# One 128-row tile of a store sent as sixteen eight-partition stores, and the closing store cut in two

## The chip, the cores and the metric

The kernel runs on one core of a Trainium2 chip. The metric is the time of one execution on the device in microseconds (us), taken from executions that are not profiled. A separate, profiled execution gave the profile and its trace; times inside it are counted from the start of its span.

## The reference

For sixteen batches the output is a scaled product plus an addend, all in float32:

```python
batch, m, k, n = 16, 512, 1024, 768
x: (16, 512, 1024)   weight: (1024, 768)   scale: 0.1   add_value: (16, 512, 768)

def reference(x, weight, scale, add_value):
    return (scale * np.matmul(x, weight) + add_value).astype(np.float32)
```

Flattened, that is 8192 rows of x against one weight matrix. The kernel moves 33.6 MB of x, 25.2 MB of addend, 3.1 MB of weight and 25.2 MB of output.

## The kernel before

**Tiles.** The 8192 rows are 64 tiles of 128 rows. Row `g*2048 + p*16 + t` lies on partition `p` of tile `16*g + t`, so that n neighbouring tiles of one group of sixteen are, on each partition, one contiguous run in DRAM: 3072 B of output or addend for each tile, 4096 B of x. The function `rows(view, s, n)` gives that slice for tiles s to s+n-1.

**Buffers.** `xs` holds 16 tiles of x. `ao` holds 32 tiles in which the addend arrives and in which the output is formed in place; tile t lies in slot `(t + 8) % 32`, so that tiles 56 to 63 take the slots of tiles 24 to 31. `mm` is four PSUM tiles.

**Compute.** ScalarE and GpSimd (`mover`, line 147) cast x to bf16 in blocks, into two buffers `va` of four tiles each. VectorE (`turn`, line 162) transposes them into `xt`, two tiles at a time. TensorE (`product`, lines 195 and 197) multiplies each tile in eight steps of K. VectorE (`finish`, line 171) takes a pair of products from PSUM, scales them, adds the addend and writes the result to `ao`; it adds 2 to the semaphore `made`. VectorE works through groups of eight tiles, four pairs each; the last group is written out behind the loop.

**Transfers.** All DMAs are issued by SyncE's queue (SP), in the order that the list `STREAM` gives: `("x", s, n)` loads n tiles of x from tile s on, `"a"` the addend, `"w"` the weight, and `"o"` stores the output. Ahead of each transfer SP waits for what that transfer needs:

- an x load waits until ScalarE and GpSimd have moved the tiles whose slots it overwrites (`by_act`, `by_pool`);
- an addend load that begins a group of eight waits for the addend load before it (`a_sem`), and one that overwrites slots of the output waits until that store has landed (`o_sem`, line 115);
- a store waits for the store two ahead of it, and for `made` (lines 125 and 126).

The store of the last eight tiles stands outside the list, at line 237, behind the critical section that holds everything else:

```python
    s, n = LAST
    nc.sync.dma_start(rows(out_v, s, n), ao[:, slot(s):slot(s) + n, :])
```

The order of work around the change is therefore the order of `STREAM`, written out by hand: one queue, served in order by the core's 16 DMA engines.

Of the kernel before, what the change touches and what calls it, by code (L numbers as in the profile page):

```python
# [8 lines left out]
P = 128  # L9
# [18 lines left out]
]  # L28
FIRST, LAST = (0, 8), (56, 8)


@with_exitstack
def kernel(
# [17 lines left out]
    T = M // P  # L51
# [5 lines left out]
    out_v = out_f.rearrange("(g p t) n -> p g t n", p=P, t=R)  # L57
    w_v = weight.rearrange("(c p r) n -> p c (r n)", p=P, r=2)

    def rows(view, s, n):  # L60
        assert s // R == (s + n - 1) // R
        return view[:, s // R, s % R:s % R + n, :]
# [5 lines left out]
    ao = const.tile([P, A_SLOTS, N], fp32, name="ao")  # L68
# [6 lines left out]
    x_sem = [tc.alloc_semaphore(f"x{i}") for i in range(X_SLOTS // MOVE)]  # L75
    a_sem, a_late = (tc.alloc_semaphore(n) for n in ("a", "a_late"))
    o_sem = [tc.alloc_semaphore(f"o{i}") for i in range(2)]
    by_act, by_pool, pool_go, turned, casts, done, made = (
        tc.alloc_semaphore(name)
        for name in ("by_act", "by_pool", "pool_go", "turned", "casts", "done", "made"))  # L80
    TURNED = MOVE * VA_BUFS
    MADE = TURNED + 2 + MM_BUFS - 2

    def slot(t):
        return (t + G) % A_SLOTS

    def sync_engine(eng):
        loads, stores, known = [], [], {}

        def need(sem, value):  # L90
            if known.get(sem, 0) < value:
                eng.wait_ge(sem, value)
                known[sem] = value

        for op, s, n in STREAM:
            last = s + n - 1
            if op == "w":
                dst = ao[:, s:s + n, :].rearrange("p (c r) n -> p c (r n)", r=2)
                move, sem = eng.dma_start(dst, w_v[:, s // 2:(s + n) // 2, :]), w_sem[s // 4]
            elif op == "x":  # L100
                k = s % X_SLOTS
                if last >= X_SLOTS:
                    moved = 8 * (last + 1 - X_SLOTS) // MOVE
                    need(by_act, moved)
                    need(by_pool, moved)
                move = eng.dma_start(xs[:, k:k + n, :], rows(x_v, s, n))
                sem = x_sem[k // MOVE]
            elif op == "a":
                if loads and s % G == 0:
                    need(a_sem, 16 * len(loads))  # L110
                if slot(s) == 0:
                    need(casts, KJ)
                if s >= A_SLOTS:
                    i = next(j for j, (a, b) in enumerate(stores) if a <= s - A_SLOTS < a + b)
                    need(o_sem[i % 2], 16 * (i // 2 + 1))
                move = eng.dma_start(ao[:, slot(s):slot(s) + n, :], rows(add_v, s, n))
                if s % G:
                    sem = a_late
                else:
                    sem = a_sem  # L120
                    loads.append((s, n))
            else:
                i = len(stores)
                if i > 1:
                    need(o_sem[i % 2], 16 * (i // 2))
                need(made, MADE + last + 1)
                move = eng.dma_start(rows(out_v, s, n), ao[:, slot(s):slot(s) + n, :])
                sem = o_sem[i % 2]
                stores.append((s, n))
            move.then_inc(sem, 16)  # L130
            if op == "x" and n == 2 * MOVE:
                eng.sem_inc(x_sem[k // MOVE + 1], 16)
# [90 lines left out]
    s, n = FIRST  # L223
# [4 lines left out]
    with tc.tile_critical(no_gpsimd_drain=True):  # L228
        sync_engine(nc.sync)
        mover(nc.scalar, nc.scalar.copy, 0, by_act)  # L230
        nc.scalar.addr_align(HALF_BLOCK, offset=PAST)
        mover(nc.gpsimd, nc.gpsimd.tensor_copy, 1, by_pool, pool_go)
        nc.gpsimd.addr_align(HALF_BLOCK, offset=PAST)
        vector_engine(nc.vector)
        tensor_engine(nc.tensor)
    s, n = LAST
# [36 lines left out]
```

## Time and profile before

| What | Value |
|---|---|
| Time, median of 3 runs | 209.35 us (209.29 to 209.39) |
| Profiled execution, span from its first to its last instruction | 207.5 us |
| Median of the runs less that span | 1.85 us |
| Bytes moved by DMA | 87.06 MB, 420 GB/s over the span |
| TensorE matmul, busy | 168.4 us, 81% of the span |
| ScalarE, GpSimd, VectorE, busy | 134.7, 135.4, 97.8 us |
| Mean granted TensorE clock | 0.975 |

The profile gives no time of its own for the profiled execution other than its span. The 1.85 us between the span and the median lie around the span (start and end of an execution); the text takes them as fixed, so that an end that moves by d in the trace is taken to move the time by d.

How to read it: busy times are of the engine, without its waits. A matmul row's time is modelled, so a busy TensorE is not TensorE at its peak. The DMA share is the mean busy share of the 16 DMA engines; a row of a table by windows counts a DMA packet wholly in the window in which it starts, so that a share can exceed 1. "us to landing" counts from the issue of a DMA to its last completion.

### The profile page before, as it was taken

What the parts mean: (1) busy time and instruction counts of PE and PEld (TensorE: products, weight loads), DVE (VectorE), ACT (ScalarE), POOL (GpSimd) and SP (SyncE); (2) the same over time, 40 slices, a digit from 0 to 9 for tenths busy, and PEclk for the clock granted to TensorE, in tenths of its full rate; (3) what the DMA queues carried; (4) which work ended last, traced back from release to release, by engine and by line L of the source; (5) the groups of instructions that cost most, each with busy time, mean ns of one, the idle gap of its engine ahead of it and who ended that gap; (6) DMA issues with size and microseconds to landing.
All of it is one profiled execution on the core that took longest, in us unless ns stands there. A gap on an engine that the chain in (4) does not pass through costs nothing.

```text
span 207.5 us, 2310 instructions
## 1 busy us (share of the span) xinstructions
PE 168.4 (81%) x1024; PEld 50.3 (24%) x512; DVE 97.8 (47%) x66; ACT 134.7 (65%) x129; POOL 135.4 (65%) x132
## 2 busy tenths in 40 slices
PE   0000099999999999999999999999999999999400
PEld 0000023333332222222233333333333333333100
DVE  0005525537555555555555554755555555553300
ACT  2059970799999796969696079999970999300000
POOL 0049994799999996969696079999990899400000
PEclk9999999999999999999999999999999999999955
DMA  7999999999999999999999999999999999999993
GB/s 291 417 381 469 403 466 404 455 455 404 404 467 442 411 398 486 393 441 407 445 436 423 423 436 455 411 445 412 441 414 422 437 445 455 460 417 388 412 441 171
DMA packets 4147, 87.06 MB, mean 420 GB/s; under 512 B 432, under 2 KB 432, under 8 KB 944
## 3 DMA queue, kind: packets, MB, share of 16 engines
q1 hardware_dynamic: 4144, 87.03, 98.1%
q14 instruction: 3, 0.02, 0.0%
HBM read 61.87 MB, written 25.17 MB: 419 GB/s over the span
## 4 chain that ended last, share of the span: by engine, by line
PE 81%; DMA 6%; ACT 5%; DVE 1%; issue 1%; DVEq 0%; ACTq 0%
PE mm L197 81%; DMA xs<-in_x_dram 6%; ACT va L147 5%; DVE ao L171 1%; DVE xt L162 1%; ACTq L140 0%; DVEq L160 0%; DVEq L168 0%
## 5 line engine op out<-in xcount | busy, mean ns | idle before, releaser
L197 PE MATMUL mm<-w_bf,xt 128*128 128x512 bf16 (+1 forms) x1024 | 168.4, 328 | 26.0 <-DVE xt L162 26.0
L147 POOL CAST va<-xs 32x1024 bf16<-32x1024 f32 x128 | 135.2, 1056 | 43.1 <-DMA xs<-in_x_dram 24.7
L147 ACT CAST va<-xs 32x1024 bf16<-32x1024 f32 x128 | 133.4, 1042 | 42.1 <-DMA xs<-in_x_dram 25.8
L171 DVE SCALAR_TENSOR_TENSOR ao<-mm,ao 128x1536 f32 (+1 forms) x32 | 56.3, 1758 | 76.5 <-PE mm L197 76.5
L195 PEld LDWEIGHTS <-xt 128*128 128x128 bf16 x512 | 50.3, 98 | 143.6 <-issue 117.6
L162 DVE STREAM_TRANSPOSE xt<-va 128x1024 f32<-128x1024 f32 x32 | 39.4, 1234 | 3.8 <-ACT va L147 2.1
L155 DVE CAST w_bf<-ao 128x3072 bf16<-128x3072 f32 x2 | 4.5, 2240 | 18.1 <-DMA ao<-in_weight_dram 18.1
L136 ACT ACT_TABLE_LOAD x1 | 1.3, 1283 | 1.3 <-SPq L228 1.3
L254 POOL MEMSET const-float32-0.0<- 128x1 f32 x1 | 0.1, 98 | 0.2 <-issue 0.2
L254 POOL MEMSET const-bfloat16-1.0<- 128x1 bf16 x1 | 0.1, 100 | 0.0
L254 POOL MEMSET const-float32-1.0<- 128x1 f32 x1 | 0.1, 98 | 0.0
L254 POOL MEMSET const-uint8-127<- 128x1 uint8 x1 | 0.1, 97 | 0.0
## 6 DMA issues: line engine op xcount, KB each, us to landing
xs<-in_x_dram SPq DMA_DIRECT2D x7, 4096.0 KB, 20.9
ao<-in_add_value_dram SPq DMA_DIRECT2D x7, 3072.0 KB, 17.0
out_dram<-ao SPq DMA_DIRECT2D x6, 3072.0 KB, 27.0
out_dram<-ao SPq DMA_DIRECT2D x1, 6144.0 KB, 35.4
xs<-in_x_dram SPq DMA_DIRECT2D x2, 2048.0 KB, 19.1
ao<-in_weight_dram SPq DMA_DIRECT2D x2, 1536.0 KB, 16.8
ao<-in_add_value_dram SPq DMA_DIRECT2D x2, 1536.0 KB, 14.9
```

The costliest lines, as they stand in the source:

```text
L136: eng.preload_act_table(mybir.ActivationFunctionType.Copy)
L147: copy(va[q % VA_BUFS][32 * b:32 * b + 32, :, a, :], src[32 * a:32 * a + 32, :, b, :]).then_inc(count, 1)
L155: eng.tensor_copy(w_bf[:, s:s + n, :], ao[:, s:s + n, :]).then_inc(casts, n)
L162: eng.transpose(xt[:, 2 * half:2 * half + 2, :, :].rearrange("p i c m -> p (i c m)"), va[move % VA_BUFS][:, q:q + 2 * KC, :, :].bitcast(fp ...
L171: eng.scalar_tensor_tensor(a, mm[:, q:q + 2, 0:N], float(scale), a, op0=mybir.AluOpType.mult, op1=mybir.AluOpType.add).then_inc(made, 2)
L195: eng.ldweights(x_j, tile_position=(0, 0))
L197: m = eng.add_instruction(mybir.InstMatmult(start_tensor_calc=(j == 0), stop_tensor_calc=(j == KJ - 1), tile_size=(P, P), tile_position=(0 ...
L254: nc = _bacc.Bacc("TRN2", target_bir_lowering=False, num_devices=1)
```

## The change

Three things change in what SP issues.

The store of tiles 24 to 31 becomes a store of tiles 24 to 30 (as before, 128 partitions) and, directly behind it, sixteen stores (`"few"`) that together hold tile 31. Each of the sixteen takes eight partitions, four apart: q, q+4, ..., q+28, for q in 0 to 3, 32 to 35, 64 to 67 and 96 to 99. They count on a semaphore of their own, `few_sem`.

The addend load of tiles 56 to 63, which overwrites the slots of tiles 24 to 31, waits also for `few_sem`.

The closing store of tiles 56 to 63 becomes two: tiles 56 to 59 at the end of `STREAM`, as soon as `made` allows, on a semaphore `end_sem`, and tiles 60 to 63 at line 237's place.

```diff
-    ("a", 40, 8), ("x", 48, 8), ("o", 16, 8), ("o", 24, 8), ("a", 48, 4), ("x", 56, 4),
-    ("a", 52, 4), ("x", 60, 4), ("a", 56, 8), ("o", 32, 16), ("o", 48, 8),
+    ("a", 40, 8), ("x", 48, 8), ("o", 16, 8), ("o", 24, 7), ("few", 31, 1), ("a", 48, 4),
+    ("x", 56, 4), ("a", 52, 4), ("x", 60, 4), ("a", 56, 8), ("o", 32, 16), ("o", 48, 8),
+    ("o", 56, 4),
 ]
-FIRST, LAST = (0, 8), (56, 8)
+FIRST, LAST = (0, 8), (60, 4)
+FEW, STEP = 8, 4
...
+    few_sem, end_sem = (tc.alloc_semaphore(name) for name in ("few", "end"))
...
                     need(o_sem[i % 2], 16 * (i // 2 + 1))
+                    if s + n == T:
+                        need(few_sem, 16 * P // FEW)
...
+            elif op == "few":
+                need(made, MADE + last + 1)
+                for p in range(0, P, FEW * STEP):
+                    for q in range(p, p + STEP):
+                        part = slice(q, q + (FEW - 1) * STEP + 1, STEP)
+                        eng.dma_start(rows(out_v, s, n)[part], ao[part, slot(s):slot(s) + n, :]
+                                      ).then_inc(few_sem, 16)
+                continue
+            elif last == T - LAST[1] - 1:
+                need(made, MADE + last + 1)
+                move = eng.dma_start(rows(out_v, s, n), ao[:, slot(s):slot(s) + n, :])
+                sem = end_sem
             else:
```

The compute engines' programs are the same.

## The prediction

> **What bounds the kernel now.** I read the page's chain and DMA sections first, then the chain in order of time, and last the end of the trace by windows.
>
> ```profile
> span 207.5 us, 2310 instructions
> PE 81%; DMA 6%; ACT 5%; DVE 1%; issue 1%; DVEq 0%; ACTq 0%
> DMA  7999999999999999999999999999999999999993
> q1 hardware_dynamic: 4144, 87.03, 98.1%
> q14 instruction: 3, 0.02, 0.0%
> ...
> 26.01 168.37 PE mm L197 x1024
> ...
> 194.48 1.76 DVE ao L171
> ```
>
> The chain says TensorE: it runs without a pause from 26.01 to 194.38 us, and one `finish` ends at 196.24. But the chain stops there, and the span goes on for 11.3 us. The DMA rows tell why: the 16 engines are busy for 98.1% of the span. Two resources are full together, and the one that ends last is the DMA queue. So what counts is when the last of the 16 DMA engines is through with its share.
>
> ```profile
> 196.53 0.33 SPq L237 DMA_DIRECT2D out_dram<-ao  x1
> ...
> out_dram<-ao SPq DMA_DIRECT2D x1, 3072.0 KB, 10.1
> ...
> 196.50:197.35 0.85, 0.00 (x0) 0.00 (x0) 0.00 (x0) 0.00 (x0) 0.00 (x0) 0.75 0.48 202
> 197.35:197.75 0.40, 0.00 (x0) 0.00 (x0) 0.00 (x0) 0.00 (x0) 0.00 (x0) 0.50 1.87 799
> 203.70:203.90 0.20, 0.00 (x0) 0.00 (x0) 0.00 (x0) 0.00 (x0) 0.00 (x0) 0.50 2.58 1106
> 203.90:204.10 0.20, 0.00 (x0) 0.00 (x0) 0.00 (x0) 0.00 (x0) 0.00 (x0) 0.50 1.14 492
> 204.10:204.35 0.25, 0.00 (x0) 0.00 (x0) 0.00 (x0) 0.00 (x0) 0.00 (x0) 0.50 0.68 295
> 204.35:205.20 0.85, 0.00 (x0) 0.00 (x0) 0.00 (x0) 0.00 (x0) 0.00 (x0) 0.50 0.01 0
> 205.20:205.60 0.40, 0.00 (x0) 0.00 (x0) 0.00 (x0) 0.00 (x0) 0.00 (x0) 0.50 0.14 61
> ...
> DMA packets 16, 0.17 MB, mean 202 GB/s; under 512 B 9, under 2 KB 9, under 8 KB 9
> ...
> DMA packets 2, 0.02 MB, mean 11 GB/s; under 512 B 1, under 2 KB 1, under 8 KB 1
> ```
>
> The first two rows are SP's issue of the closing store and its landing, 10.1 us later, at 206.6. The last two numbers of a window row are the DMA share and GB/s, and a packet counts where it starts. From 203.70 to 204.35 there start 1106 x 0.20 + 492 x 0.20 + 295 x 0.25 = 393 KB, sixteen packets of 24,576 B (eight tiles of one partition), in 16 x (2.58 x 0.20 + 1.14 x 0.20 + 0.68 x 0.25) = 14.6 us: 0.914 us each. Then no data packet starts until 205.20, and then a single one (61 x 0.40 = 24 KB). The last row says the same of 205.2 to the end: two packets, one of data and one of under 512 B, the semaphore write. So **one engine is a whole packet behind the others**: fifteen end between 204.6 and 205.2, the sixteenth at 205.2 + 0.9 = 206.1, and the landing at 206.6 is that one's.
>
> The same engine was late already before the closing store. Its eight packets took 8 x 0.914 = 7.3 us, so it began them at 198.8. The next to last row shows the others: of 16 packets between 196.50 and 197.35 nine are semaphore writes, so nine engines were through with the store before; in the next 0.40 us 799 x 0.40 = 320 KB, 13 packets, start together, where an undisturbed queue starts 16 x 0.40 / 0.914 = 7. Those nine stood idle until the closing store reached them, about 0.8 us after its issue; the late one never did.
>
> **The closing store in two.** Tiles 56 to 59 need two pairs of the last group.
>
> ```profile
> 158.23 1.76 DVE L171 SCALAR_TENSOR_TENSOR ao<-mm,ao 128x1536 f32 x1 [2.41 <-PE mm L197]
> ...
> 178.91 1.76 DVE L171 SCALAR_TENSOR_TENSOR ao<-mm,ao 128x1536 f32<-128x1536 f32 x1 [2.28 <-PE mm L197]
> ...
> 184.08 1.76 DVE L171 SCALAR_TENSOR_TENSOR ao<-mm,ao 128x1536 f32<-128x1536 f32 x1 [2.26 <-PE mm L197]
> ...
> SPq L228 <- DVEq L228: 20.3, 1, 20.3
> ```
>
> The second pair is made at 185.84. SP would issue then, in the middle of a wait of 20.3 us in which it has nothing else to do; behind it in SP stands only the end of the section, which waits for the pair at 196.24 anyway. The bytes are the same. What goes is the idle time: the 1.5 MB of tiles 56 to 59 wait in the queue when the store before ends near 197, and keep each engine for 3.7 us, long past the 0.8 us that the closing store needs to arrive. Nine engines gain up to 0.85 us (I take 0.3, since thirteen packets starting inside 0.40 us leave little room for more on average); the late engine gains nothing. **By itself this part moves the end by 0.**
>
> **The sixteen small stores.** In the trace a 128-partition DMA leaves 128 data packets and 16 semaphore writes (25 such and two weight loads of 256 + 16 are the 4144 packets), so a DMA's rows are dealt out over the engines, eight to each. Eight partitions are eight rows, and can occupy at most eight engines. Which eight, no run shows yet. [...]
>
> ```profile
> 13.50:19.50 6.00, 0.00 (x0) 0.00 (x0) 2.31 (x1) 5.85 (x7) 5.76 (x5) 1.00 1.02 428
> 113.50:144.50 31.00, 31.00 (x193) 9.37 (x96) 17.35 (x13) 23.55 (x23) 22.70 (x22) 1.00 0.99 426
> ```
>
> The price of a 3072 B packet: the weight's 6144 B packets ran at 428 / (16 x 1.02) = 26.2 GB/s, 0.234 us each; with 0.914 us for 24,576 B that is 0.037 us per KB and about 0.008 us for each packet. So 3072 B cost 0.121 us, and a semaphore write some 0.009 us (window 204.35 to 205.20: share 0.01 x 0.85 us x 16 for fifteen). If the same eight engines always serve, each **loaded** engine takes 16 x (0.121 + 0.009) = 2.08 us in place of 8 x 0.113 = 0.90 us: **+1.18 us**. Each of the other eight is **relieved** by **0.90 us**. Bounds: nothing is gained below the 0.113 us of bytes alone (+0.90), and an upper bound is in the rivals.
>
> ```profile
> 113.20 0.84 SPq L127 DMA_DIRECT2D out_dram<-ao  x2
> 144.95 0.34 SPq L116 DMA_DIRECT2D ao<-in_add_value_dram  x1
> ...
> 156.18 0.33 SPq L116 DMA_DIRECT2D ao<-in_add_value_dram  x1
> 156.56 19.29 SPq L127 DMA_DIRECT2D out_dram<-ao  x2
> ...
> SPq L92 <- DMA out_dram<-ao: 30.8, 1, 30.8
> ...
> ao<-in_add_value_dram SPq DMA_DIRECT2D x1, 3072.0 KB, 20.9
> ```
>
> On SP sixteen more issues at 0.4 us are 6.7 us, from 114 to 121. There SP waits 30.8 us for a store to land, and issues the next load at 144.95; the cover would hold up to 1.9 us an issue. The tile waits for no more than the store of 24 to 31 did. The wait on `few_sem` stands before the load issued at 156.18; everything ahead of that load's predecessor in the queue is through by then, so it costs nothing. Behind the small stores the loaded engines deliver the loads 1.18 us later. The addend for tile 48 has landed by 156.18 and is used at 158.23: 2.0 us to spare. That for tile 56 lands at 156.18 + 20.9 = 177.1 and is used at 178.91: 1.8 us. Both cover 1.18; without that cover TensorE would be held up only after `finish` has lost the rest of a 5.2 us pair.
>
> **The sum.** If the late engine is a relieved one, it ends at 206.1 - 0.9 = 205.2. Of the others nine end at 204.6 to 204.8 now (9 packets start from 203.70 to 203.90), 204.4 without the idle time; a loaded one of these ends at 204.4 + 1.18 = 205.6. The other six end at 204.8 to 205.2, and loaded at 206.0 to 206.4. With the bulk of nine loaded, the end moves from 206.1 to 205.6 or 205.7, by 0.45 us: 207.5 becomes 207.05 and 209.35 becomes **208.9**. The floor is the relieved late engine, 0.9 less, 208.45.
>
> ```profile
> 1.70:1.90 0.20, 0.00 (x0) 0.00 (x0) 0.00 (x0) 0.20 (x1) 0.00 (x0) 1.00 4.73 1311
> 1.90:2.70 0.80, 0.00 (x0) 0.00 (x0) 0.00 (x0) 0.73 (x1) 0.00 (x0) 1.00 1.03 328
> ```
>
> Why relieved? At the first load eight engines start within 0.2 us (1311 x 0.20 = 262 KB, eight packets of 32 KB) and the other eight over the next 0.8 us. That looks like work dealt out in a fixed order, half by half. [...]
>
> **The rivals.** **Late engine among the loaded:** it then carries 206.1 + 1.2 = 207.3, and the time is 210.55, slower. It decides from the first small store on; for it speaks that either half may hold the late engine, against it only the order of the start. **Room too small:** one of the six later engines is loaded and ends at 206.0 to 206.4, about where the late one does now: 209.25 to 209.65, say 209.45, no change. For it speak the three instruction packets of the q14 row, which hold up single engines wherever they fall. **No shift:** the rows go to the engines that serve these partitions anyway; each engine pays 8 x 0.13 - 0.90 = +0.14, 209.5, and the change doesn't rebalance at all. **Dear small stores:** if a loaded engine had to wait for each small store to land before the next, at 0.5 us each (landing 206.6 against 206.1), that is 16 x 0.5 = 8 us more, an end at 205.6 + 8 = 213.6, and 216.9. It turns slower from (206.5 - 203.5) / 16 = 0.19 us for each small store on, against my 0.13 (203.5 being a loaded engine's end without tile 31). Against it: 27 DMAs follow each other in a queue that is 98.1% busy, so a boundary costs next to nothing, though none here had packets this short. [...]
>
> **How the numbers follow.** Forecast 0.40; late engine loaded 0.22; room too small 0.18; no shift 0.10; dear small stores 0.10. A measurement here can tell about 0.2%, 0.42 us, from no change. Faster by more: the forecast, 0.40. Within: room too small and no shift, 0.28. Slower: 0.22 + 0.10 = 0.32. The range from 208.4 to 210.6 takes in all but the dear stores and some tails; the forecast's own is 208.4 to 209.2.
>
> **What would show it.** In the changed profile: 128 more small packets of under 512 B for the sixteen stores if eight engines each signal once, and 128 more data packets under 8 KB; TensorE still without a pause up to about 194.4; SP's small issues between 114 and 121; the store of tiles 56 to 59 issued near 186 and no starved window near 197. Right is the forecast if the last engines end near 205.6 in a group and no single packet follows by itself. A lone engine 2 us behind the rest tells of the first rival; eight engines ending over 206.5 together, of dear small stores; two groups absent and the lone one unchanged, of no shift. I am wrong altogether if matmuls pause behind the small stores.

## The result

The changed kernel takes 210.81 us (210.69 to 211.21) against 209.32 us (209.23 to 209.39) before, in runs side by side: a ratio of 1.0078 with a 95% interval of 1.0066 to 1.0090. It is **slower by 1.49 us**. The forecast was 208.9, and the range ended at 210.6.

The profiled execution took 210.92 us with a span of 209.0, so 1.9 us lie around it, as before. Its page, against the lines shown of before:

```profile
span 209.0 us, 2327 instructions
...
DMA packets 4547, 87.06 MB, mean 417 GB/s; under 512 B 576, under 2 KB 576, under 8 KB 1216
q1 hardware_dynamic: 4544, 87.03, 97.6%
...
PE 81%; DMA 6%; ACT 5%; DVE 1%; issue 1%; DVEq 0%; ACTq 0%
```

The chain of waits still names TensorE and ends long before the span does. The bytes are the same to two digits; the time that the 16 DMA engines share fell from 98.1% to 97.6% of a longer span. The packets carry the first finding: 576 of under 512 B, where the 432 of before and 16 for the second closing store would be 448. The other 128 are semaphore writes of the sixteen small stores, eight for each. **A store of eight partitions ran on eight engines.**

The end by windows (granted TensorE clock, DMA share, GB/s are the last three numbers), and the last 1.9 us of the DMA section:

```profile
197.00:198.25 1.25, 1.00 1.01 433
203.00:203.50 0.50, 0.50 1.04 442
203.50:204.20 0.70, 0.50 0.66 281
204.40:205.32 0.92, 0.50 0.50 214
205.50:206.20 0.70, 0.50 0.41 176
206.20:207.10 0.90, 0.50 0.10 41
207.10:207.60 0.50, 0.50 0.06 25
...
DMA packets 2, 0.01 MB, mean 6 GB/s; under 512 B 1, under 2 KB 1, under 8 KB 1
```

Up to 203.5 all engines work. Then the share falls to 0.50 and stays there: eight engines are through by about 204.2, before any engine was in the kernel before, and eight work on to 206 and later. The window from 207.10 shows one packet of 12,288 B by itself (25 GB/s x 0.50 us), which starts at 207.15 and takes 0.46 us: one engine is again last, now to 207.6 instead of 206.1. That is the whole loss: 1.5 us. It stands in the slow half, not in the relieved one.

SP did what it was meant to do:

```profile
114.97 10.84 SPq L132 DMA_DIRECT2D out_dram<-ao  x16
145.16 0.35 SPq L121 DMA_DIRECT2D ao<-in_add_value_dram  x1
...
186.75 0.33 SPq L137 DMA_DIRECT2D out_dram<-ao  x1
197.41 0.33 SPq L254 DMA_DIRECT2D out_dram<-ao  x1
```

The sixteen issues took 10.8 us, and SP then still waited until 145.16. The first part of the close went out at 186.75, ten us ahead of the rest.

TensorE's last product came 0.9 us later than before, but that is not the loss. The delay is there already at 101 us, before SP reaches anything new, as the same `finish` shows in the timelines of before and after:

```profile
100.92 1.76 DVE L171 SCALAR_TENSOR_TENSOR ao<-mm,ao 128x1536 f32 x1 [2.17 <-PE mm L197]
101.80 1.76 DVE L188 SCALAR_TENSOR_TENSOR ao<-mm,ao 128x1536 f32 x1 [2.17 <-PE mm L214]
```

In the first experiment with the small stores alone the last `finish` starts 0.4 us earlier than in the kernel before, and that kernel loses as much.

### The profile page after: what moved, and what is told of

The parts are those of the page before. It is cut to its first block, busy times and chain, and to the rows that moved or that the text cites. A ratio compares the mean times of both kernels' runs of the same rounds, so it can differ in the third digit from the quotient of the medians.

```text
span 209.0 us, 2327 instructions
## 1 busy us (share of the span) xinstructions
PE 169.2 (81%) x1024; PEld 50.5 (24%) x512; DVE 97.9 (47%) x66; ACT 134.7 (64%) x129; POOL 135.4 (65%) x132
## 3 DMA queue, kind: packets, MB, share of 16 engines
q1 hardware_dynamic: 4544, 87.03, 97.6%
## 4 chain that ended last, share of the span: by engine, by line
PE 81%; DMA 6%; ACT 5%; DVE 1%; issue 1%; DVEq 0%; ACTq 0%
PE mm L214 81%; DMA xs<-in_x_dram 6%; ACT va L164 5%; DVE ao L188 1%; DVE xt L179 1%; ACTq L157 0%; DVEq L177 0%; DVEq L185 0%
## 5 line engine op out<-in xcount | busy, mean ns | idle before, releaser
L214 PE MATMUL mm<-w_bf,xt 128*128 128x512 bf16 (+1 forms) x1024 | 169.2, 329 | 26.1 <-DVE xt L179 26.1
```

What stands on the lines that cost most here:

```text
L214: m = eng.add_instruction(mybir.InstMatmult(start_tensor_calc=(j == 0), stop_tensor_calc=(j == KJ - 1), tile_size=(P, P), tile_position=(0 ...
```

## The experiments

Theory A: the DMA engine that ends last is among those that the small stores load. Theory B: the short stores themselves are dear, wherever they go. Theory C: the cut of the close, or what it does to SP, costs the time.

### One part at a time

Only the cut (the wait on `few_sem` goes too):

```diff
-("o", 24, 7), ("few", 31, 1), ("a", 48, 4),
+("o", 24, 8), ("a", 48, 4),
```

> Only the closing store is cut in two; tile 31 goes with its eight-tile store as before. If the late DMA engine sets the end (theory A: it never stood idle, and the sixteen small stores load it), this gives 209.3 within 0.15 us of before, a single packet still ending by itself near 206.1, and no starved stretch near 197. If the time of the change came from the cut (rival: an additional store, a later close), 210.5 or more.

Measured: 209.28 against 209.24, ratio 1.0003 (0.9994 to 1.0012).

```profile
203.80:204.80 1.00, 0.50 0.78 332
204.80:205.80 1.00, 0.50 0.12 49
205.80:206.40 0.60, 0.50 0.00 0
...
DMA packets 2, 0.01 MB, mean 6 GB/s; under 512 B 1, under 2 KB 1, under 8 KB 1
```

The last line is the stretch from 205.6 on: one data packet and its semaphore write. The last engine ends at 206.1 with the cut as without it. The cut is worth nothing by itself, and theory C falls.

Only the small stores:

```diff
-    ("o", 56, 4),
-FIRST, LAST = (0, 8), (60, 4)
+FIRST, LAST = (0, 8), (56, 8)
```

> Only the sixteen small stores; the closing store stays whole. Theory A: all of the loss is here, 210.6 to 210.9, and the late engine ends near 207.6 as in the changed kernel, since it finds the closing store waiting with or without the cut. Rival, the loss comes from the cut: 209.3.

Measured: 210.77 against 209.24, ratio 1.0079 (1.0065 to 1.0092). The sixteen stores hold all of the loss.

```profile
194.06 1.76 DVE L187 SCALAR_TENSOR_TENSOR ao<-mm,ao 128x1536 f32<-128x1536 f32 x1 [3.44 <-PE mm L213]
```

That is its last `finish`, with TensorE on time.

### The same short packets, spread evenly

```diff
-                for p in range(0, P, FEW * STEP):
-                    for q in range(p, p + STEP):
-                        part = slice(q, q + (FEW - 1) * STEP + 1, STEP)
...
+                parts = [slice(q, P, 8) for q in range(8)]
+                for part in parts:
```

> Tile 31 goes in eight stores of sixteen partitions instead of sixteen of eight: the same 128 packets of 3072 B, 128 semaphore writes, but one row for each of the 16 engines. Theory A (the shift of load is what costs): every engine takes 8 x 0.13 - 0.90 = 0.14 us more, 209.3 to 209.6. Rival, short stores are dear wherever they go: half of the changed kernel's small packets on each engine, so half of its loss, 210.0 or more.

Measured: 209.94 against 209.24, ratio 1.0037 (1.0024 to 1.0050): between the two. I suspected the choice of partitions and tried another list:

```diff
+                parts = [slice(q, q + 106, 7) for q in range(7)] + [slice(112, 128)]
```

> Again eight stores of sixteen partitions for tile 31, now seven partitions apart (the last sixteen side by side), where the earlier ones were eight apart. If that kernel's 0.7 us came from the partitions it put side by side in time (eight apart: few of them distinct by fours), this gives 209.3 to 209.5; if it came from the short stores reaching the late engine at all, 209.8 or more again.

Measured: 209.84 against 209.35, ratio 1.0023 (1.0010 to 1.0037). The two intervals overlap, so the choice of partitions is not shown to matter. The profile of the second counts 576 packets under 512 B, 448 and sixteen for each of the eight stores, so all engines serve each. Evenly spread, the short packets cost 0.5 to 0.7 us, where the shift of load is gone and the packets as priced are worth 0.14. A holds for the larger part of the loss. Some 0.35 to 0.55 us are left that it does not explain; whether the short stores themselves take it (B) is answered below, under "What a short store costs".

### How far the first k engines reach

If a store of k partitions always takes the same first k engines, then stores of other widths find the late engine. First eighteen stores of seven partitions:

```diff
+                parts = [slice(q, q + 109, 18) for q in range(18)] + [slice(126, 128)]
```

> Tile 31 goes in eighteen stores of seven partitions, 18 apart, and one of two. If a store of k partitions always uses the first k engines and the late one is the eighth, it is now relieved by 0.9 us and ends near 205.3; the seven loaded ones take 18 or 19 x 0.13 - 0.90 = 1.5 us more and end at 206.0 to 206.8: 209.2 to 210.0. If the late one is among the first seven, it ends 0.3 us later than in the changed kernel: 211.1. If short stores are dear in themselves: 211.0 or more, in a group of seven.

Measured: 211.20 against 209.24, ratio 1.0092 (1.0077 to 1.0106). That fits a late engine among the first seven (211.1), but dear short stores as well (211.0 or more). Then a part of the tile as one store, and the rest in eight stores of two, four and six partitions (the list `parts` of each kernel):

```diff
+ two:   [slice(0, 112)] + [slice(q, q + 5, 4) for q in (112, 113, 114, 115, 120, 121, 122, 123)]
+ four:  [slice(0, 96)] + [slice(q, q + 13, 4) for q in (96, 97, 98, 99, 112, 113, 114, 115)]
+ six:   [slice(0, 80)] + [slice(q, q + 41, 8) for q in range(80, 88)]
```

> Of tile 31, 112 partitions go in one store (seven rows for each of 16 engines), the last sixteen in eight stores of two. If a store of k partitions uses the first k engines, two engines take 8 x 0.13 - 0.11 = 0.93 us more and fourteen 0.11 less. Late engine one of the first two: 210.2. Not: 209.2 (the late one still ends last, 0.1 us earlier; the loaded two stay below it). If it is short stores as such that cost: 209.9, half of the changed kernel's loss for half of its stores.

> The same with 96 partitions in one store and eight stores of four. Four engines take 8 x 0.13 - 0.23 = 0.81 us more, twelve 0.23 less. Late engine among the first four: 210.1. Not: 209.0. Short stores as such: 209.9.

> The same with 80 partitions in one store and eight stores of six. Six engines take 8 x 0.13 - 0.34 = 0.70 us more, ten 0.34 less. Late engine among the first six: 210.0. The seventh: 208.9. Short stores as such: 209.9.

Measured: 209.98, 210.53 and 210.53 against 209.35; ratios 1.0037 (1.0023 to 1.0050), 1.0064 (1.0050 to 1.0078), 1.0065 (1.0052 to 1.0079). As times these miss what A expected for an engine that isn't loaded (209.2, 209.0), so times alone would mislead. The windows near the end say more. These rows are of the stores of two, four, six and seven, in this order; each is 0.92 us long, two packets of the last store, so that 16 times its share is the number of engines still at work:

```profile
205.00:205.92 0.92, 0.50 0.19 80
...
204.80:205.72 0.92, 0.50 0.31 134
...
204.50:205.42 0.92, 0.50 0.38 160
...
204.60:205.52 0.92, 0.50 0.44 187
```

16 x 0.19 = 3, 16 x 0.31 = 5, 16 x 0.38 = 6, 16 x 0.44 = 7, and in the changed kernel 16 x 0.50 = 8. After stores of two and of four there is one engine more than the stores load; after stores of six, seven and eight there is none more. So the late engine lies outside the first four and inside the first six, if a wider store takes the engines of a narrower one and more, which these counts agree with and don't prove.

### Load alone

To take the short packets out of the question, one additional store of PAD partitions behind that of tiles 24 to 31, in the kernel with only the cut. It copies 24,576 B from each of these partitions once more, to a spare place in DRAM, which adds 0.92 us to PAD engines:

```diff
+            elif op == "pad":
+                part = slice(0, 4 * PAD - 3, 4)
+                eng.dma_start(spare[0:PAD, :, :], ao[part, slot(s):slot(s) + n, :]).then_inc(few_sem, 16)
```

> The kernel with only the closing store cut in two, plus one more store right behind that of tiles 24 to 31: four partitions (four apart), 24,576 B each, copied once more to a spare place in DRAM. It adds work and takes none away: 0.92 us on as many engines as it has partitions, in one long packet each, with no short stores. If the late engine is not among the first four (the stores of four left five engines late, the loaded four and one more): 209.3, at most 209.6, since the loaded four have 0.6 to 1.2 us of room. If it is: 210.2.

> The same with five partitions. If the late engine is the fifth: 210.2. If it is the sixth: 209.3 to 209.6, as with four.

> The same with eight partitions. If the loss of the changed kernel is load on the first eight engines, the late one among them, 0.92 us of load without any short store gives 210.2, and the profile ends with one engine alone near 207.0. If it was the short stores themselves, 209.3.

Measured against 209.24: with four partitions 209.70, ratio 1.0022 (1.0013 to 1.0031); with five 210.22, 1.0047 (1.0034 to 1.0061); with eight 210.22, 1.0051 (1.0037 to 1.0064).

From five to eight nothing changes, and both lose 0.98 us, the price of the load. The fifth engine sets the end, and three more loaded engines don't. With four the loss is half, a little more than was allowed for the loaded engines running out of room; that it is one of these which ends last there is argued, not shown. The ends of the three kernels, four, five and eight in this order:

```profile
205.80:206.40 0.60, 0.50 0.05 20
206.40:206.90 0.50, 0.50 0.00 0
...
205.80:206.40 0.60, 0.50 0.15 61
206.40:206.90 0.50, 0.50 0.06 25
...
205.80:206.40 0.60, 0.50 0.10 41
206.40:206.90 0.50, 0.50 0.06 25
```

With four, one packet starts after 205.80 and none after 206.40; with five and eight one more starts after 206.40, alone. On the condition above, **the late engine is the fifth** that a store takes, counted from the first, and load on it moves the end about one for one: 0.98 us for 0.92.

### An attempt to relieve it

Tiles 29 to 31 as one store of 112 partitions and four stores of four, 9216 B each, meant to let the first four engines take work from the other twelve:

```diff
-("o", 24, 7), ("few", 31, 1)
+("o", 24, 5), ("few", 29, 3)
+                parts = [slice(0, 112)] + [slice(q, q + 13, 4) for q in range(112, 116)]
```

> An attempt at relief of the late engine with few and longer packets: tiles 24 to 28 as one store, tiles 29 to 31 as one store of 112 partitions and four stores of four partitions (9216 B each). Twelve engines take 0.35 us less, the first four 4 x 0.355 - 0.35 = 1.07 us more. If the late engine is not among the first four and the price holds: it ends 0.35 us earlier, the loaded four at 205.4 to 206.2: 208.9 to 209.3. If short or misplaced packets cost the loaded engines as much over their price as in the stores of four (about 1.5 us): 209.9.

Measured: 211.53 against 209.24, ratio 1.0114 (1.0098 to 1.0129), far above both. The idea of relief by narrow stores failed here, for a reason that isn't shown: this kernel shares with the stores of two, four and six a store of less than 128 partitions, and all four lose more than the price of the late engine's load: 0.63, 1.18, 1.18 and 2.29 us (two, four, six, this one), where the expectations, with that engine as the fifth, have it at 0.11 and 0.23 less, 0.70 more and 0.35 less.

### What a short store costs

Open was the rest: 1.49 us lost where the load explains 1.2. Sixteen short stores of five partitions, 3072 B from each, in place of the one additional store, from partitions 0 to 19 and then from 64 to 83:

```diff
+                for j in range(2 * n):
+                    q = 0 + j % 4        # second kernel: 64 + j % 4
+                    part = slice(q, q + 4 * PAD - 3, 4)
+                    eng.dma_start(spare[0:PAD, j, :], ao[part, slot(s) + j // 2, :]).then_inc(few_sem, 16)
```

> As the kernel with one additional store of five partitions, but the additional work goes in sixteen stores of five partitions, four apart, of 3072 B each, from partitions 0 to 19: 16 x 0.13 = 2.08 us more on the first five engines, nothing taken off. If a short store costs the late engine its 0.13 us: 209.28 + 2.1 = 211.4. If shortness costs it more (the changed kernel lost 0.3 us over the price of its load): 211.7 or more.

> [...] If it doesn't matter whose partitions an engine reads: as from partitions 0 to 19, within 0.2 us. [...]

Measured: 211.82 and 211.50 against 209.30; ratios 1.0118 (1.0101 to 1.0135) and 1.0107 (1.0090 to 1.0124). Whose partitions they are makes no difference that these runs show; if anything those from 64 to 83 are cheaper.

By the times, sixteen short stores cost 2.2 to 2.5 us, 0.14 to 0.16 each. The traces show that the stores themselves take less. The first two lines are of the changed kernel, from 152.40 to 153.27 and from 157.30 to 157.32; the last two are of the kernel with one additional store of five partitions, from 152.98 to 153.01 and from 156.67 to 156.70:

```profile
DMA packets 40, 0.35 MB, mean 403 GB/s; under 512 B 7, under 2 KB 7, under 8 KB 13
DMA packets 3, 0.03 MB, mean 1639 GB/s; under 512 B 1, under 2 KB 1, under 8 KB 1
...
DMA packets 3, 0.02 MB, mean 819 GB/s; under 512 B 1, under 2 KB 1, under 8 KB 1
DMA packets 3, 0.03 MB, mean 1092 GB/s; under 512 B 1, under 2 KB 1, under 8 KB 1
```

Packets under 512 B are semaphore writes: with one, each engine ends its part of a DMA (432 for the 27 DMAs of the kernel before, 16 for each). In the first stretch the late engine is by itself with its last short stores: seven of them in 0.87 us, **0.124 us each**, no more than the prediction's 0.13. The last of its semaphore writes there is at 153.26. The next one, behind the load of tiles 48 to 51 (eight packets of 12,288 B), is at 157.31, 4.05 us later; those of the other engines for this load come before 156.42. With one long additional store in place of the short ones the same load takes it 156.69 - 153.00 = 3.69 us, the eight packets' own 0.46 us each. So 0.36 us of the loss arise **in the load right behind the short stores**. The sixteen stores of five partitions show the same, 4.07 us from 154.15 to 158.22. For the changed kernel the sum is 16 x 0.124 - 0.90 + 0.36 = 1.44 us; measured were 1.49.

The excess is not always in that place. In the profile of the eight stores of sixteen partitions (an execution of 210.59 us) the late engine's load behind them takes 3.65 us, and instead one packet of 21,504 B, just ahead of the small stores, takes 11.81 x 0.01 us x 16 = 1.9 us, where others of its size take 0.80:

```profile
150.57:150.59 0.01, 1.00 11.81 2151
```

So theory B holds in another form: the short stores are not dear themselves, but packets next to them in the queue took longer in these profiles, by 0.36 us in the load behind or by 1.1 us in the packet ahead. Why, no run shows.

## Why the prediction was wrong

**What bounds the kernel: right.** The DMA engine that ends last sets the time: 206.1 and 209.32 us before, 207.6 and 210.81 after. The cut alone left that engine and the time where they were (206.1, 209.28), and with one more loaded engine, the fifth, the loss was about the size of its load (0.98 us for 0.92).

**The cut in two: right.** It was taken at nothing, for the late engine began the closing store at 198.8, when this had reached the others at about 197.35, and gave 1.0003. In the changed kernel the starved stretch near 197 is gone (share 1.01); with the cut alone the share from 196.40 to 197.80 is 0.82, the same as before. Either way, engines that gain there don't decide.

**Eight engines for each small store, the same ones: right.** 128 more semaphore writes, and two groups of eight at the end (share 0.50 from 204.40 to 205.32). The counts 3, 5, 6, 7, 8 agree, as far as they go, with wider stores that take the same engines and more. Which of the sixteen these are, no run shows: the views give engines no numbers.

**SP: covered, though the issue was mis-priced.** It cost 0.68 us for each small store instead of 0.4, and 10.8 of the 30 us were there to be used. The loads behind held up no product: TensorE's only wait in the profile is its first, of 26.1 us.

**Which half the late engine is in: the step that failed.** The forecast took the late engine for a relieved one, with the order of the start in the first load as its ground, and gave that 0.40 against 0.22. No run shows that the engines that start late are those that a store of eight partitions leaves out. The runs showed the late engine as the fifth, and the small stores loaded it. The order of the start was no evidence, for the gap at the end is not that old. These are stretches of the kernel before, 77.70 to 78.30, 136.80 to 136.90, 150.60 to 151.45 and 151.90 to 152.00:

```profile
DMA packets 32, 0.52 MB, mean 874 GB/s; under 512 B 16, under 2 KB 16, under 8 KB 16
DMA packets 4, 0.05 MB, mean 492 GB/s; under 512 B 2, under 2 KB 2, under 8 KB 2
DMA packets 40, 0.32 MB, mean 376 GB/s; under 512 B 15, under 2 KB 15, under 8 KB 15
DMA packets 6, 0.06 MB, mean 614 GB/s; under 512 B 1, under 2 KB 1, under 8 KB 1
```

At 78 us all sixteen engines write their semaphore for the same load within 0.6 us. At 136.9 the last two of another load still come within 0.1 us of each other. At the end of the store of tiles 24 to 31 fifteen are through by 151.45 and one comes by itself, near 152.0. Half of the gap of 0.9 us thus arose while the stores of tiles 16 to 31 were served, and the rest later; why in that engine, no run shows. Without the order of the start, the two halves were even.

**The room of the other loaded engines: mis-sized too.** The sum had nine loaded engines end near 205.6 and the others by 206.4. The changed kernel from 206.13 to 206.90:

```profile
DMA packets 8, 0.04 MB, mean 48 GB/s; under 512 B 5, under 2 KB 5, under 8 KB 5
```

Five loaded engines besides the late one end in this stretch, the last of them close to 206.9. With the late engine in the other half they alone would have held the end 0.8 us later than before: some 210.1, an estimate from this trace. The forecast of 208.9 needed more than the right half; the rival "room too small" saw this, but with 209.65 at most.

**The rival that came true was named, with its sign and its place, at 210.55.** It ended at 210.81, 0.2 us outside the range. The price of a short store was right: 0.13 expected, 0.124 in the trace. The term that was missing is the 0.36 us in the load behind them. The prediction put it at nothing, as "a boundary costs next to nothing", and said itself that no packets so short had been seen.

**Dear small stores: wrong as a wait for each landing** (216.9), and by far so: no 0.5 us for each. Queued behind other work, the sixteen stores took the late engine 2.0 us (16 x 0.124), and 0.36 behind them.

No kernel here is faster than the one before.

## What to carry to other kernels

Here the DMA engines were busy for 98.1% of the span, the time was that of one engine (206.1, the next at 205.2), and a change in how rows are dealt out was worth what it did to that engine, not to the mean: with the same bytes, 1.49 us lost. Where a trace shows such an end, find out which engine it is before moving load: one additional store of k partitions told it here in three runs (k of 4, 5 and 8: 209.70, 210.22, 210.22 us), while the order in which engines start did not. Find out also since when it is late: the gap at the end was not one of the start (at 136.9 the last two engines were still within 0.1 us of each other). Cutting the closing store was worth nothing (1.0003), for the engine that ends last had not stood idle before it.

## What the runs showed of the hardware

One DMA engine, the fifth if wider stores take the engines of narrower ones and more, ends 0.9 us behind the next one (206.1 against 205.2). Half of that arose between 136.9 and 152.0, around two stores; why, no run shows. A store of eight partitions takes SP 0.63 to 0.80 us to issue; the six stores of the list in the kernel before, of 128 partitions, took 0.34 to 0.43:

```profile
L132 SPq DMA_DIRECT2D out_dram<-ao x16: 625/626/800, 115.0 to 125.2; - x16
...
L127 SPq DMA_DIRECT2D out_dram<-ao x6: 344/398/426, 73.1 to 175.5; - x6
```

A store of 3072 B rows took the late engine 0.124 us in the queue, where the forecast priced its packet and its semaphore write at 0.121 and 0.009. Behind sixteen such stores the late engine needed 4.05 and 4.07 us, in two profiles, for a load that took 3.69 without them; in a third, with eight such stores, 3.65. Why stays open. Stores of 80, 96 and 112 partitions with narrow ones behind them cost 0.6 to 2.3 us; what in them costs it stays open.
